# One unbroken run for the 32 narrow matmuls of each group of heads in a Mamba-2 stage

## The chip, the cores and the metric

The kernel runs on one core of a Trainium2 chip. The time is the device time of one launch in microseconds (us). A kernel is timed in several runs, and the median counts. One more execution, of the same program, is recorded by the hardware profiler; all rows below come from that record.

The engines are named as in the profile: PE is TensorE (the matmuls; PEld is its loading of weights), DVE is VectorE, ACT is ScalarE, POOL is GpSimd, SP is SyncE, which issues the DMAs here. Each engine takes its instructions in the fixed order of its own queue and waits at a semaphore where an operand or a buffer isn't ready.

## The reference

A two-layer decoder trunk on 256 tokens of width 2048, in f32. The first layer mixes with a Mamba-2 SSD block, the second with dilated sliding-window attention. Only the SSD block is touched:

```python
proj = h @ in_w
z, xBC, dt = split(proj)
xBC = silu(causal_depthwise_conv(xBC))          # width 4
xs, Bm, Cm = split(xBC)                          # 64 heads of 64, 8 groups, state 128
dt = softplus(dt + dt_bias);  A = -exp(A_log)
acum = cumsum(dt * A)                            # one chunk of 256 tokens
decay = exp(where(causal, acum[:, :, None] - acum[:, None, :], -inf))
cb = einsum("blgn,bsgn->blsg", Cm, Bm)
y = einsum("blsgk,bsgkp->blgkp", cb[..., None] * decay, xs * dt)
y = (y + xs * D_skip) * silu(z)
y = y * rsqrt(mean(y**2 per group) + eps) * norm_g
return y @ out_w
```

## The kernel before

The 256 tokens are two blocks of 128 (b = 0, 1). The 64 heads are eight groups of eight heads, g = 0 to 7. Every large product is made in f32 by three matmuls: ACT copies a weight piece of 128x1024 from `raw` to a rounded `whi` (L100), DVE makes the rest `wlo` = raw - whi (L102), and PE multiplies activation and weight in the combinations whi x hi, wlo x hi and whi x lo (L151 to L153, L182/L185, L213 to L215, three ways of tiling). The pieces arrive by DMA from SP's queue; `whi` and `wlo` have four buffers each.

The loop over the groups interleaves two things. For group g+1 it makes the projections ("bc" for every second group, "xs" for x, "z" for the gate). For group g it runs three steps:

- `stage1(g)`: two scores matmuls per group (L720, L721) into a PSUM tile `aux`, masked on DVE to `cb` (L723, L724). For each half of the heads (w = 0, 1) the rows of cumulated decay are fetched by DMA to `cbc`, ACT makes eight `Relu` (L734) and one `Exp` (L736) into `seg`, and DVE multiplies `seg` by `cb` (L737). PE transposes x (L745, four at a time, into an `aux` tile per block), and DVE makes from it `xd` (x times dt, L747), the skip term in `y` (L750) and, for block 0, `xo` (L755).
- `stage2(g)`: one matmul `po` = cb x xo (L767) into an `aux` tile. DVE scales it (L768) and adds it to y (L770). Then for each block b an output tile `py`, and for each of the eight heads two matmuls of 64 columns (L776): 32 such operations in all, each of them two records in the trace. DVE adds py to y (L777) and multiplies by the gate (L778); ACT squares with an accumulated sum (L779); DVE turns the sums into a factor (L781, L253 to L259).
- `stage3(g)`: ACT scales y by that factor (L787).

`y_tiles(g)` transposes the finished y (L829 on PE, into `aux` tiles) for the output projection, with L833 on ACT and L834 on DVE. The DVE also works through a background job, `ada_dot` (L295, one pass over 128x2048), which has nothing to do with the groups.

Buffers: `aux` (PSUM) two; `py` (PSUM) two; `seg`, `cbc` and `cb` two each; `xd` and `xo` one. So a `seg` of group g+1 can be written only when the py matmuls of group g have read it.

The order on each engine is not that of the source. A scheduler places every instruction by its priority and by estimates of when its operands are ready. `tc.issue_after(i)` obliges an instruction to be issued behind i; `tc.high_priority(n)` lifts its priority by n. Apart from these, an instruction of another product may slip between two of a loop, which is why the 32 matmuls of a group are cut in places by L213 to L215 or other work.

Of the kernel before, what the change touches and what calls it, by code (L numbers as in the profile page):

```python
# [9 lines left out]
F32 = mybir.dt.float32  # L10
# [8 lines left out]
P = 128  # L19
# [5 lines left out]
HPG = 8  # L25
# [24 lines left out]
def trunk(ctx, tc, xT, x, c, par, cst, bias, lnrow, ada, wdt, win, wxs, wout, wk, wv, wbin, wbout, out):  # L50
    nc = tc.nc
    V, S, T, PO = nc.vector, nc.scalar, nc.tensor, nc.gpsimd
# [196 lines left out]
    def rsqrt(v, tag):  # L249

        y = sm.tile(list(v.shape), F32, name=tag + "y")
        sh = sm.tile(list(v.shape), I32, name=tag + "s")
        V.tensor_scalar(sh, v.bitcast(I32), 1, None, op0=ALU.logical_shift_right)  # L253
        V.tensor_tensor(y.bitcast(I32), magic[:, :v.shape[1]], sh, op=ALU.subtract)
        t = sm.tile(list(v.shape), F32, name=tag + "t")
        for _ in range(3):
            V.tensor_tensor(t, y, y, op=ALU.mult)
            V.scalar_tensor_tensor(t, t, -0.5, v, op0=ALU.mult, op1=ALU.mult)
            V.scalar_tensor_tensor(y, t, 1.5, y, op0=ALU.add, op1=ALU.mult)  # L259
        return y  # L260
# [73 lines left out]
    with ExitStack() as cA:  # L334
# [15 lines left out]
        with ExitStack() as cS:  # L350
# [327 lines left out]
            aux2 = cS.enter_context(tc.tile_pool(name="aux2", bufs=2, space=PSUM, reuse_waits="tile"))  # L678
# [83 lines left out]
            def stage2(g, segs, xd, cb, xo):  # L762

                ss = sm.tile([P, 2], F32, name="ss")

                po = aux.tile([P, 512], F32, name="aux")
                T.matmul(po, cb[:, 2, :], xo, start=True, stop=True)  # L767
                V.tensor_tensor(xo.rearrange("p (h e) -> p h e", h=HPG), po.rearrange("p (h e) -> p h e", h=HPG),  # L768
                                dec[:, 1, g * HPG:(g + 1) * HPG, None].to_broadcast([P, HPG, 64]), op=ALU.mult)
                V.tensor_tensor(y[g][:, 1, :], xo, y[g][:, 1, :], op=ALU.add)  # L770
                for b in range(2):
                    py = aux2.tile([P, 512], F32, name="py")
                    for hh in range(HPG):
                        e_ = slice(64 * hh, 64 * hh + 64)
                        for t_ in (slice(0, 64), slice(64, 128)):
                            T.matmul(py[t_, e_], segs[hh // 4][:, hh % 4, b, t_], xd[:, b, e_], start=True, stop=True)  # L776
                    V.tensor_tensor(y[g][:, b, :], py, y[g][:, b, :], op=ALU.add)  # L777
                    V.tensor_tensor(y[g][:, b, :], y[g][:, b, :], sz[g][:, b, :], op=ALU.mult)  # L778
                    S.activation(py, y[g][:, b, :], AF.Square, accum_out=ss[:, b:b + 1])  # L779
                ms = sm.tile([P, 2], F32, name="ms")  # L780
                V.tensor_scalar(ms, ss, 1.0 / 512, EPS, op0=ALU.mult, op1=ALU.add)  # L781
                return rsqrt(ms, "a")
# [66 lines left out]
            product("z", G - 1, last_product)  # L849
            drain()  # L850
            stage3(G - 1, stage2(G - 1, *st1))
        aux = ctx.enter_context(tc.tile_pool(name="auxb", bufs=2, space=PSUM, reuse_waits="tile"))

# [197 lines left out]
    aux2 = ctx.enter_context(tc.tile_pool(name="aux3", bufs=2, space=PSUM))  # L1051
# [220 lines left out]
    _, r1, step = root(1, between)  # L1272
# [7 lines left out]
    for n, h0, h1 in ((0, 0, 512), (1, 0, 512), (3, 0, 512), (2, 0, 256), (2, 256, 512)):  # L1280
        c = slice(512 * n + h0, 512 * n + h1)
        with tc.issue_after(step.ins):
            step = V.scalar_tensor_tensor(u[1][:, c], cen[n][:, h0:h1] if n < 3 else u[1][:, c], r1, lnt[:, 1, c],
                                          op0=ALU.mult, op1=ALU.add)
# [93 lines left out]
```

## Time and profile before

| | us |
|---|---|
| median of 3 runs | 1233.01 (1232.63 to 1233.83) |
| profiled execution, its time | 1234.53 |
| its span, first to last instruction | 1232.7 |
| mean granted TensorE clock | 0.999 |
| PE busy in the span | 1216.1 (99%) |
| DVE busy | 1026.8 (83%) |
| ACT busy | 700.3 (57%) |
| SSD groups, first to last py matmul (L776) | 229.5 to 515.6 |

A row of the timeline gives the start and the duration in us, the engine, the line, the operation, out<-in with tile names, the shape and how many rows of one kind follow each other (x64); where the engine sat idle before it, the idle time and the releaser stand in brackets at the end. A row of DVE or ACT that stands for several has their common duration. Consecutive matmuls overlap in the records, so the price of one is read from start to start. In the table of windows each engine has its busy us in the stretch and the number of records.

### The profile page before, as it was taken

How to read it: one execution, taken by the hardware profiler on the slowest of the kernel's cores; microseconds unless marked ns; L12 is line 12 of the kernel's file. 1: busy time of each engine (PE TensorE's matmuls, PEld its weight loads, DVE VectorE, ACT ScalarE, POOL GpSimd, SP SyncE). 2: the span in 40 equal slices, each digit the busy share in tenths (PEclk: the TensorE clock that was granted, in tenths of full speed). 3: DMA queues.
4: the chain of work that ended last, by engine and by line, in shares of the span. 5: the costliest groups of instructions: out<-in, count | busy, mean ns of one | idle time of the engine just before them, and what ended most of it. 6: DMA issues, size and time to landing. Idle time of an engine off the chain costs nothing.

```text
span 1232.7 us, 18854 instructions
## 1 busy us (share of the span) xinstructions
PE 1216.1 (99%) x7132; PEld 1045.7 (85%) x7132; DVE 1026.8 (83%) x1464; ACT 700.3 (57%) x1048; POOL 3.9 (0%) x8
## 2 busy tenths in 40 slices
PE   8899999999999999999999999999999999999998
PEld 7889988798888888888888788888888888888886
DVE  6999986999988989899778678888978866758776
ACT  4555476878597789754435545344445644445551
POOL 0000000000000000000000000000000000000001
PEclk9999999999999999999999999999999999999999
DMA  9999976686666456599988569989997784464673
GB/s 376 423 420 423 421 256 240 217 304 242 228 207 205 169 172 207 197 339 353 362 314 302 199 204 351 357 346 371 389 395 296 228 258 150 122 197 129 206 257 69
DMA packets 81371, 335.92 MB, mean 273 GB/s; under 512 B 9200, under 2 KB 9984, under 8 KB 68480
## 3 DMA queue, kind: packets, MB, share of 16 engines
q1 hardware_dynamic: 80352, 333.33, 74.9%
q0 software_dynamic: 576, 1.05, 0.6%
q8 instruction: 56, 0.92, 0.3%
q10 hardware_dynamic: 352, 0.34, 0.1%
q14 instruction: 35, 0.29, 0.1%
HBM read 331.45 MB, written 3.23 MB: 271 GB/s over the span
## 4 chain that ended last, share of the span: by engine, by line
PE 82%; DMA 7%; DVE 6%; ACT 3%; issue 2%; ACTq 0%; DVEq 0%; SPq 0%
PE acc L182 24%; PE acc L185 12%; PE acc L214 12%; PE acc L215 11%; PE acc L213 11%; DMA raw<-in_win 5%; DVE wlo L102 2%; DVE araw L295 2%; PE py L776 1%; ACT whi L100 1%; PE acc L151 1%; PE acc L153 1%; PE acc L152 1%; PE acc L986 1%; DMA raw<-in_wv 1%
## 5 line engine op out<-in xcount | busy, mean ns | idle before, releaser
L100 ACT ACTIVATE whi<-raw 128x1024 fp32r<-128x1024 f32 x389 | 408.2, 1058 | 350.4 <-PE acc L215 127.1
L102 DVE TENSOR_TENSOR wlo<-raw,whi 128x1024 fp32r<-128x1024 f32 x389 | 468.7, 1220 | 148.2 <-ACT whi L100 140.9
L182 PE MATMUL acc<-actT,whi 128*128 128x512 f32 x1280 | 400.8, 393 | 0.0
L185 PEld LDWEIGHTS acc<-actT,wlo 128*128 128x128 f32 x1280 | 239.3, 188 | 52.3 <-DVE wlo L102 0.7
L214 PE MATMUL acc<-wlo,actT 128*128 128x512 f32 x656 | 257.4, 392 | 2.2 <-DVE wlo L102 2.2
L185 PE MATMUL acc<-actT,wlo 128*128 128x256 f32 x1280 | 254.0, 280 | 0.0
L213 PE MATMUL acc<-whi,actT 128*128 128x512 f32 x656 | 253.9, 394 | 0.0
L295 DVE SCALAR_TENSOR_TENSOR araw<-araw,cb__72 128x2048 f32<-128x2048 f32 x95 | 216.9, 2283 | 5.3 <-DMA araw<-in_ada 5.3
L182 PEld LDWEIGHTS acc<-actT,whi 128*128 128x128 f32 x1280 | 195.0, 188 | 0.4
L215 PE MATMUL acc<-whi,actT 128*128 128x512 f32 x432 | 168.8, 391 | 0.0
L214 PEld LDWEIGHTS acc<-wlo,actT 128*128 128x128 f32 x656 | 123.2, 188 | 29.5 <-DVE wlo L102 4.4
L213 PEld LDWEIGHTS acc<-whi,actT 128*128 128x128 f32 x656 | 122.6, 188 | 24.7 <-ACT s L635 0.5
L151 PE MATMUL acc<-actT,whi 128*128 128x256 f32 x372 | 103.0, 281 | 2.3 <-ACT s L635 1.3
L153 PE MATMUL acc<-actT,wlo 128*128 128x256 f32 x372 | 101.7, 281 | 1.7 <-DVE wlo L102 1.5
L152 PE MATMUL acc<-actT,whi 128*128 128x256 f32 x372 | 102.9, 279 | 0.0
L215 PEld LDWEIGHTS acc<-whi,actT 128*128 128x128 f32 x432 | 81.1, 188 | 16.6
L215 PE MATMUL acc<-whi,ylo 128*128 128x512 f32 x224 | 87.5, 391 | 0.0
L151 PEld LDWEIGHTS acc<-actT,whi 128*128 128x128 f32 x372 | 69.6, 188 | 3.6 <-ACT s L635 1.7
L153 PEld LDWEIGHTS acc<-actT,wlo 128*128 128x128 f32 x372 | 68.8, 188 | 2.9 <-DVE wlo L102 2.9
L152 PEld LDWEIGHTS acc<-actT,whi 128*128 128x128 f32 x372 | 70.6, 190 | 0.2
L215 PEld LDWEIGHTS acc<-whi,ylo 128*128 128x128 f32 x224 | 42.1, 188 | 8.4
L734 ACT ACTIVATE seg<-cbc,cumT 128x128 f32<-128x128 f32 x128 | 41.1, 389 | 4.1 <-PE py L776 2.1
(311 smaller groups left out, 1147.4 us busy)
## 6 DMA issues: line engine op xcount, KB each, us to landing
araw<-in_ada SPq DMA_DIRECT2D x96, 1024.0 KB, 7.0
raw<-in_win SPq DMA_DIRECT2D x109, 512.0 KB, 6.2
raw<-in_wout SPq DMA_DIRECT2D x64, 512.0 KB, 5.5
raw<-in_wbin SPq DMA_DIRECT2D x64, 512.0 KB, 4.3
raw<-in_wxs SPq DMA_DIRECT2D x48, 512.0 KB, 4.4
raw<-in_wv SPq DMA_DIRECT2D x48, 512.0 KB, 6.3
raw<-in_wk SPq DMA_DIRECT2D x48, 512.0 KB, 7.3
cbc<-cumd SPq DMA_DIRECT2D x16, 512.0 KB, 5.0
```

Source lines behind the costliest of these rows:

```text
L100: copied.append(S.activation(hi, raw, AF.Copy))
L102: latest.append(V.tensor_tensor(lo, raw, hi.bitcast(F32), op=ALU.subtract))
L151: T.matmul(o, hi[:, k, c_], ahi[:, kt, :], start=first, stop=False, skip_group_check=True)
L152: T.matmul(o, hi[:, k, c_], alo[:, kt, :], start=False, stop=False, skip_group_check=True)
L153: T.matmul(o, lo[:, k, c_], ahi[:, kt, :], start=False, stop=kt == k1 - 1, skip_group_check=True)
L182: T.matmul(ps[n], hi[:, k, n * P:n * P + P], both(kt), start=kt == 0, stop=False, skip_group_check=True)
L185: T.matmul(ps[n][:, 0, :], lo[:, k, n * P:n * P + P], high(kt), start=False, stop=kt == KT - 1, skip_group_check=True)
L213: T.matmul(o, h_, hi[:, k, :], start=kt == k0, stop=False, skip_group_check=part)
L214: T.matmul(o, h_, lo[:, k, :], start=False, stop=False, skip_group_check=part)
L215: end = T.matmul(o, l_, hi[:, k, :], start=False, stop=kt == k1 - 1, skip_group_check=part)
L295: return V.scalar_tensor_tensor(raw, raw, 1.0, cb_, op0=ALU.mult, op1=ALU.mult, accum_out=mod[layer][:, ct, j:j + 1])
L734: S.activation(seg[:, hh, b, :], cbc[:, hh, b, :], AF.Relu, bias=cumT[:, b, h0 + hh:h0 + hh + 1], scale=-1.0)
```

## The change

Both py tiles of a group are allocated ahead of the matmuls. The 32 matmuls are issued block 1 first, then block 0, and the heads from the last to the first. Each is obliged to come behind the one before it, the first behind the `po` matmul, and all of them have a priority raised by 400. The sums on DVE and ACT follow in the order block 1, block 0, after all matmuls have been written.

```diff
--- before.py
+++ after.py
@@ -764,16 +764,20 @@
                 ss = sm.tile([P, 2], F32, name="ss")
 
                 po = aux.tile([P, 512], F32, name="aux")
-                T.matmul(po, cb[:, 2, :], xo, start=True, stop=True)
+                step = T.matmul(po, cb[:, 2, :], xo, start=True, stop=True)
                 V.tensor_tensor(xo.rearrange("p (h e) -> p h e", h=HPG), po.rearrange("p (h e) -> p h e", h=HPG),
                                 dec[:, 1, g * HPG:(g + 1) * HPG, None].to_broadcast([P, HPG, 64]), op=ALU.mult)
                 V.tensor_tensor(y[g][:, 1, :], xo, y[g][:, 1, :], op=ALU.add)
-                for b in range(2):
-                    py = aux2.tile([P, 512], F32, name="py")
-                    for hh in range(HPG):
+                pys = {b: aux2.tile([P, 512], F32, name="py") for b in (1, 0)}
+                for b in (1, 0):
+                    for hh in reversed(range(HPG)):
                         e_ = slice(64 * hh, 64 * hh + 64)
                         for t_ in (slice(0, 64), slice(64, 128)):
-                            T.matmul(py[t_, e_], segs[hh // 4][:, hh % 4, b, t_], xd[:, b, e_], start=True, stop=True)
+                            with tc.issue_after(step.ins), tc.high_priority(400):
+                                step = T.matmul(pys[b][t_, e_], segs[hh // 4][:, hh % 4, b, t_], xd[:, b, e_],
+                                                start=True, stop=True)
+                for b in (1, 0):
+                    py = pys[b]
                     V.tensor_tensor(y[g][:, b, :], py, y[g][:, b, :], op=ALU.add)
                     V.tensor_tensor(y[g][:, b, :], y[g][:, b, :], sz[g][:, b, :], op=ALU.mult)
                     S.activation(py, y[g][:, b, :], AF.Square, accum_out=ss[:, b:b + 1])
```

The lines behind it move down: L776 becomes L777, L777 becomes L781, L778 L782, L779 L783, L781 L785, L829 L833, L833 L837, L834 L838. The instructions are the same in number, apart from two more loads of ACT's function table (the program's order has 1024 ACT instructions, it had 1022). What changes lies between group 0 and the end of group 7; ahead of it and behind it every engine's order is as before. On PE, the runs of L776 were 15 and 17 long in group 0 (po between them), 19 and 13 in group 2, 3 and 29 in groups 3 and 4, 12 and 20 in group 7, and 32 in groups 1, 5 and 6; now all eight are 32, each directly behind its po.

The first place is group 2. On PE, the po of group 2 and the products around it (acc_3338 and acc_3339 are the z projection of group 3; whi_3354, whi_3372 and whi_3390 are three of its weight pieces in turn), before:

```order
L215 MATMUL acc_3339<-whi_3372,actT_84 128x512
L213 MATMUL acc_3338<-whi_3390,actT_84 128x512
L213 MATMUL acc_3339<-whi_3390,actT_84 128x512
L767 MATMUL aux_3488<-xo_3329,cb_3292 128x512
L776 MATMUL py_3492<-xd_3321,seg_3297 64x64 x8
L776 MATMUL py_3492<-xd_3321,seg_3310 64x64 x8
L776 MATMUL py_3512<-xd_3321,seg_3297 64x64 x3
L214 MATMUL acc_3338<-wlo_3391,actT_84 128x512
L215 MATMUL acc_3338<-whi_3390,actT_84 128x512
L214 MATMUL acc_3339<-wlo_3391,actT_84 128x512
L215 MATMUL acc_3339<-whi_3390,actT_84 128x512
```

and now:

```order
L215 MATMUL acc_3339<-whi_3354,actT_84 128x512
L213 MATMUL acc_3338<-whi_3372,actT_84 128x512
L213 MATMUL acc_3339<-whi_3372,actT_84 128x512
L767 MATMUL aux_3488<-xo_3329,cb_3292 128x512
L777 MATMUL py_3492<-xd_3321,seg_3310 64x64 x8
L777 MATMUL py_3492<-xd_3321,seg_3297 64x64 x8
L777 MATMUL py_3493<-xd_3321,seg_3310 64x64 x8
L777 MATMUL py_3493<-xd_3321,seg_3297 64x64 x8
L214 MATMUL acc_3338<-wlo_3373,actT_84 128x512
L215 MATMUL acc_3338<-whi_3372,actT_84 128x512
L214 MATMUL acc_3339<-wlo_3373,actT_84 128x512
```

The po has come forward by four L213, four L214 and four L215, and the 13 matmuls that stood further down are now part of the run. On DVE in the stretch that leads to the same group's xo (xo_3329 comes further down, at the end of group 2's L747, L750 and L755; araw is the background job), before:

```order
L102 TENSOR_TENSOR wlo_3355<-raw_3352,whi_3354 128x1024
L295 SCALAR_TENSOR_TENSOR araw_3610,mod0_80<-araw_3610,cb__72 128x2048
L102 TENSOR_TENSOR wlo_3373<-raw_3370,whi_3372 128x1024
L191 TENSOR_TENSOR xs_3071<-acc_3178,xs_3071 128x256
L191 TENSOR_TENSOR xs_3071<-acc_3179,xs_3071 128x256
L723 TENSOR_TENSOR cb_3292<-aux_3289,cc_76 128x256
L368 SCALAR_TENSOR_TENSOR cacc_3275<-xs_3071,prm_74,cacc_3275 128x255
```

and now:

```order
L102 TENSOR_TENSOR wlo_3355<-raw_3352,whi_3354 128x1024
L295 SCALAR_TENSOR_TENSOR araw_3937,mod0_80<-araw_3937,cb__72 128x2048
L723 TENSOR_TENSOR cb_3292<-aux_3289,cc_76 128x256
L191 TENSOR_TENSOR xs_3071<-acc_3178,xs_3071 128x256
L191 TENSOR_TENSOR xs_3071<-acc_3179,xs_3071 128x256
L724 COPY cb_3292<-aux_3289 128x128
L737 TENSOR_TENSOR seg_3297<-seg_3297,cb_3292 128x1024
```

The piece wlo_3373 has gone behind the group's own work, and the background pass that stands here is a later one (araw_3937 for araw_3610): from group 0's L768 to the xo of group 2 there are 7 passes of L295 for 6 before, and 24 of L102 for 25. In group 1 the run with its po has gone back by 12 L182 and 10 L185 matmuls; between the L781 of group 0 and the xo of group 1, DVE has 4 L295 for 2, 14 L102 for 12, 24 L368 for 18 and 4 L191 for 2, since the two L745 blocks of that group stand later too.

The second place is the entry to group 5, on ACT (seg_4787 and seg_4800 are group 5's, py_4417 and py_4437 group 4's, whi_4584 a weight piece of the product that runs then), before:

```order
L100 ACTIVATE whi_4501<-raw_4499 128x1024
L100 ACTIVATE whi_4507<-raw_4505 128x1024
L100 ACTIVATE whi_4584<-raw_4582 128x1024
L414 ACTIVATE sz_4407<-s7_101 128x512
L734 ACTIVATE seg_4787<-cbc_4785,cumT_104 128x128
L414 ACTIVATE sz_4407<-s7_101 128x512
L734 ACTIVATE seg_4787<-cbc_4785,cumT_104 128x128 x7
L779 ACTIVATE py_4417,ss_4412<-s4_98 128x512
L779 ACTIVATE py_4437,ss_4412<-s4_98 128x512
L100 ACTIVATE whi_4606<-raw_4604 128x1024
```

and now:

```order
L734 ACTIVATE seg_4787<-cbc_4785,cumT_104 128x128 x8
L734 ACTIVATE seg_4800<-cbc_4798,cumT_104 128x128
L736 ACT_TABLE_LOAD
L736 ACTIVATE seg_4787<-seg_4787 128x1024
L414 ACT_TABLE_LOAD
L414 ACTIVATE sz_4407<-s7_101 128x512 x2
L783 ACTIVATE py_4417,ss_4412<-s4_98 128x512
L783 ACTIVATE py_4418,ss_4412<-s4_98 128x512
L365 ACTIVATE cacc_4538<-s5_99,prm_74 128x256
L365 ACTIVATE cacc_4544<-s5_99,prm_74 128x256
L365 ACTIVATE cacc_4551<-s5_99,prm_74 128x256
L100 ACTIVATE whi_4584<-raw_4582 128x1024
```

The nine Relu, the Exp and two table loads stand now ahead of whi_4584. On DVE the matching wlo_4585 has gone behind seven of the L368 (the convolution). On PE the L720, the L721 and four L745 of group 5 have come forward, to stand behind the first two L182 of whi_4584.

The third place is the passage from group 6 to group 7. On PE (aux_5309, aux_5342 and aux_5351 are group 7's scores and its two transposed blocks; acc_5275 and acc_5276 are the z projection of group 7), before:

```order
L214 MATMUL acc_5276<-wlo_5292,actT_84 128x512
L215 MATMUL acc_5276<-whi_5291,actT_84 128x512
L720 MATMUL aux_5309<-bcm_4550 128x2x128
L721 MATMUL aux_5309<-bcm_4550 128x128
L745 MATMUL aux_5342<-cc_76,xs_4950 128x128 x4
L213 MATMUL acc_5275<-whi_5360,actT_84 128x512
L214 MATMUL acc_5275<-wlo_5361,actT_84 128x512
L215 MATMUL acc_5275<-whi_5360,actT_84 128x512
L745 MATMUL aux_5351<-cc_76,xs_4950 128x128 x4
```

and now:

```order
L214 MATMUL acc_5275<-wlo_5361,actT_84 128x512
L215 MATMUL acc_5275<-whi_5360,actT_84 128x512
L767 MATMUL aux_5215<-xo_5205,cb_5168 128x512
L777 MATMUL py_5219<-xd_5197,seg_5186 64x64 x8
L777 MATMUL py_5219<-xd_5197,seg_5173 64x64 x8
L777 MATMUL py_5220<-xd_5197,seg_5186 64x64 x8
L777 MATMUL py_5220<-xd_5197,seg_5173 64x64 x8
L720 MATMUL aux_5309<-bcm_4550 128x2x128
L721 MATMUL aux_5309<-bcm_4550 128x128
L745 MATMUL aux_5342<-cc_76,xs_4950 128x128 x4
```

The run of group 6 (xd_5197) with its po has gone back by 33 matmuls (11 each of L213, L214 and L215) and stands now directly ahead of group 7's scores; before, it stood where the z projection begins. Further down, the L829 of `y_tiles(0)` (aux_5414 and aux_5423) follow each other with the first use of wlo_5397 behind them, and the 12 py matmuls of group 7 that stood between are gone from there. On ACT (seg_5317 and seg_5330 are group 7's), before:

```order
L734 ACTIVATE seg_5317<-cbc_5315,cumT_104 128x128 x6
L370 ACTIVATE xs_4950<-cacc_5151 128x256
L370 ACTIVATE xs_4950<-cacc_5157 128x256
L734 ACTIVATE seg_5317<-cbc_5315,cumT_104 128x128 x2
L734 ACTIVATE seg_5330<-cbc_5328,cumT_104 128x128
L736 ACT_TABLE_LOAD
L736 ACTIVATE seg_5317<-seg_5317 128x1024
L779 ACTIVATE py_5219,ss_5214<-s6_100 128x512
L734 ACTIVATE seg_5330<-cbc_5328,cumT_104 128x128 x3
L779 ACTIVATE py_5239,ss_5214<-s6_100 128x512
L734 ACTIVATE seg_5330<-cbc_5328,cumT_104 128x128 x4
L100 ACTIVATE whi_5396<-raw_5394 128x1024
```

and now:

```order
L100 ACTIVATE whi_5434<-raw_5432 128x1024
L734 ACTIVATE seg_5317<-cbc_5315,cumT_104 128x128 x8
L734 ACTIVATE seg_5330<-cbc_5328,cumT_104 128x128
L736 ACT_TABLE_LOAD
L736 ACTIVATE seg_5317<-seg_5317 128x1024
L783 ACTIVATE py_5219,ss_5214<-s6_100 128x512
L783 ACTIVATE py_5220,ss_5214<-s6_100 128x512
L734 ACTIVATE seg_5330<-cbc_5328,cumT_104 128x128 x7
L837 ACTIVATE xs_5412<-aux_5414,prm_74 128x256
L736 ACTIVATE seg_5330<-seg_5330 128x1024
L837 ACTIVATE xs_5412<-aux_5423,prm_74 128x256
```

whi_5396 and whi_5434 come now ahead of the nine Relu, and the Exp of seg_5330 behind an L833 (now L837). On DVE, wlo_5397 stands behind L755 of block 0 and L747 and L750 of block 1 as before, but ahead of the second L737.

## The prediction

> **What bounds the kernel.** I read the page's busy times first, then the table of windows, then what PE waits for, and last the timelines of PE, DVE and ACT around each group's narrow matmuls.
>
> ```profile
> span 1232.7 us, 18854 instructions
> PE 1216.1 (99%) x7132; PEld 1045.7 (85%) x7132; DVE 1026.8 (83%) x1464; ACT 700.3 (57%) x1048; POOL 3.9 (0%) x8
> ...
> 225.00:520.00 295.00, 295.00 (x2052) 252.12 (x2051) 273.06 (x470) 233.07 (x403) 0.00 (x0) 1.00 0.62 211
> 520.00:700.00 180.00, 179.45 (x817) 147.59 (x816) 146.72 (x180) 81.40 (x102) 0.00 (x0) 1.00 0.87 317
> 700.00:1233.00 533.00, 528.42 (x2877) 453.32 (x2875) 416.79 (x572) 254.12 (x361) 3.67 (x4) 1.00 0.73 254
> ```
>
> In the second window, where all eight groups lie, PE is busy for 295.00 of 295.00 us: it waits for nothing, so nothing that the change makes arrive earlier can shorten it. Only matmuls that get cheaper can, and every new wait of PE costs its full length, because behind 520 us PE is again busy for 707.87 of 713 us and has next to no slack to give it back. DVE, at 273.06 us, has 22 us to spare in the same window, and those are not spread evenly.
>
> **What is saved: the breaks.** The 32 operations are 64 records. Group 4 has a short piece of them and then the rest, group 6 an unbroken run:
>
> ```profile
> 414.87 1.02 PE L767 MATMUL aux<-xo,cb 128*128 128x512 f32 x2
> 415.82 0.45 PE L776 MATMUL py<-xd,seg 128*64 128x64 f32 x6
> 416.19 0.50 PE L214 MATMUL acc<-wlo,actT 128*128 128x512 f32 x1
> 416.53 0.40 PE L215 MATMUL acc<-whi,actT 128*128 128x512 f32 x1
> 416.77 0.40 PE L214 MATMUL acc<-wlo,actT 128*128 128x512 f32 x1
> ...
> 418.40 0.40 PE L215 MATMUL acc<-whi,actT 128*128 128x512 f32 x1
> 418.72 1.96 PE L776 MATMUL py<-xd,seg 128*64 128x64 f32 x58
> ...
> 485.80 2.09 PE L776 MATMUL py<-xd,seg 128*64 128x64 f32 x64
> 487.82 0.50 PE L213 MATMUL acc<-whi,actT 128*128 128x512 f32 x1
> ```
>
> The 64 of group 6 take 2.02 us from start to start of what follows, 32 ns each. The plain pace of a 512-wide matmul is 0.23 to 0.24 us (416.53 to 416.77). The last L215 ahead of the second piece takes 0.32 (418.40 to 418.72), the L214 behind the first 0.34 (416.19 to 416.53), and the six records take 0.37 (415.82 to 416.19) where 6 x 0.032 is 0.19. So a break costs 0.09 ahead, 0.11 behind and 0.10 to 0.18 in the piece, 0.30 to 0.38 us. The upper end counts the start of a run as well, which stays, so I take 0.30. Four pieces merge (groups 2, 3, 4 and 7): 4 x 0.30 = **1.2 us** saved, at most 1.5. Group 0's break by its po (15 and 17) is worth 0.1 to 0.2, and the L721 that the new order puts far behind its L720 costs about as much; I set both to nothing. Reversing heads and blocks changes neither number nor shape: nothing.
>
> The Trainium skill, page "TensorEngine Tiling (Array Packing)", section Key Properties, says that changing the tiling mode drains TensorE, and gives no figure. The trace agrees in kind: the L214 behind a piece takes 0.34 us. By that rule the gain would be what the rows give, 1.2 us, or more if a drain is hidden from them, which is a rival below.
>
> **What is added: waits.** The raised priority places a whole run where one piece stood, and moves others. I went through each group and asked whether xo (for the po) and the weight pieces behind the run are there.
>
> *Groups 1 and 2.*
>
> ```profile
> 246.16 0.17 DVE L781 TENSOR_SCALAR ms<-ss 128x2 f32<-128x2 f32 x1 [0.94 <-ACT py L779]
> 246.24 2.29 DVE L295 SCALAR_TENSOR_TENSOR araw<-araw,cb__72 128x2048 f32<-128x2048 f32 x1
> ...
> 278.02 0.68 DVE L755 TENSOR_TENSOR xo<-aux,dec 128x512 f32<-128x512 f32 x1
> ...
> 317.76 0.68 DVE L755 TENSOR_TENSOR xo<-aux,dec 128x512 f32<-128x512 f32 x1
> ...
> 319.55 4.62 DVE L102 TENSOR_TENSOR wlo<-raw,whi 128x1024 fp32r<-128x1024 f32 x4
> ...
> 324.98 1.23 DVE L102 TENSOR_TENSOR wlo<-raw,whi 128x1024 fp32r<-128x1024 f32 x1 [0.21 <-ACT whi L100]
> ...
> 485.74 0.76 DVE L191 TENSOR_TENSOR xs<-acc,xs 128x256 f32<-128x256 f32 x2
> ...
> 487.01 2.44 DVE L368 SCALAR_TENSOR_TENSOR cacc<-xs,prm,cacc 128x255 f32<-128x255 f32 x6
> ...
> 283.46 1.02 PE L767 MATMUL aux<-xo,cb 128*128 128x512 f32 x2
> 318.99 1.02 PE L767 MATMUL aux<-xo,cb 128*128 128x512 f32 x2
> ```
>
> Between 246.16 and 324.98 DVE has no bracket of idle time: 79 us in which its times are sums of its own work. Up to group 2's xo the new order gives it one L295 more (2.28) and one L102 less (4.62 / 4 = 1.15): xo ends at 318.44 + 1.13 = 319.6. The wait of 0.94 us at 246.16 is for an L779, which in the new order stands ahead of three Relu (0.3 each) and not behind them; it may end 0.85 earlier, and then xo at 318.7. PE reaches that po twelve 512-wide matmuls earlier, at 318.99 - 12 x 0.23 = 316.2. The wait is 2.5 to 3.4 us. I take **2.6**, near the lower end, since the order does have that L779 ahead. Up to 1.1 of it falls to group 1 already: there DVE has two L295, two L102, six L368 and two L191 more ahead of xo (4.6 + 2.3 + 2.4 + 0.7 = 10.0; 278.70 becomes 288.6, or 287.8), and PE comes 12 L182 and 10 half as wide L185 later (2.8 + 1.2; 283.46 becomes 287.4). The two waits are one: DVE is behind by what it is behind at group 2, and PE loses it there or earlier.
>
> *Groups 0, 3, 4 and 6.* Group 0's run has no piece ahead of the po any more and waits 0.1 for xo. In 3 and 4 the order ahead of the po is unchanged, and PE didn't wait there. In 6 the po comes 33 matmuls later (7.6 us, at 492.4) and xo, on DVE, at 492 by the same kind of sum. I take **0.1** in all.
>
> *Group 5's entry.*
>
> ```profile
> 421.12 2.15 ACT L734 ACTIVATE seg<-cbc,cumT 128x128 f32<-128x128 f32 x7
> 423.18 0.58 ACT L779 ACTIVATE py<-s 128x512 f32<-128x512 f32 x1
> ...
> 425.47 1.28 ACT L736 ACT_TABLE_LOAD   x1
> 426.76 1.06 ACT L736 ACTIVATE seg<-seg 128x1024 f32<-128x1024 f32 x1
> 427.73 1.57 ACT L365 ACTIVATE cacc<-s,prm 128x256 f32<-128x256 f32 x3
> ...
> 428.93 0.62 PE L182 MATMUL acc<-actT,whi 128*128 128x512 f32 x2
> 429.39 0.40 PE L185 MATMUL acc<-actT,wlo 128*128 128x256 f32 x2
> ...
> 493.41 0.59 PE L720 MATMUL aux<-bcm 128*128 128x256 f32 x2
> ...
> 494.42 0.48 PE L213 MATMUL acc<-whi,actT 128*128 128x512 f32 x1
> ```
>
> The run of group 4 ends near 417.8 (414.87 + 0.95 + 2.0) and frees its seg. From there ACT has nine Relu (2.7), two table loads (2.6), an Exp (1.0), two L414 (1.0, of L779's shape), two L779 (1.2), three L365 (1.5) and then the copy whi_4584 (1.0): 11.0 us, to 428.8, where PE wants it at 428.93 less the 0.3 of a break saved. On DVE wlo_4585 now stands behind seven L368, which begin when the first L365 ends, near 426.9: 2.8, small steps 0.5, itself 1.15, so it ends at 431.3. PE wants it at 429.39, later by the 1.0 of the L720, L721 and four L745 put ahead of it (493.41 to 494.42), earlier by the 0.3: 430.1. I take **1.0**, since ACT costs PE 0.1 to 0.2 of that before; 0.6 to 1.9 as ends, by whether L365 comes on time.
>
> *Group 7.* This is the largest term.
>
> ```profile
> 487.47 1.87 ACT L734 ACTIVATE seg<-cbc,cumT 128x128 f32<-128x128 f32 x6 [0.18 <-PE py L776]
> ...
> 497.34 0.68 DVE L755 TENSOR_TENSOR xo<-aux,dec 128x512 f32<-128x512 f32 x1
> ...
> 500.55 1.22 DVE L102 TENSOR_TENSOR wlo<-raw,whi 128x1024 fp32r<-128x1024 f32 x1
> ...
> 500.88 0.60 PE L829 MATMUL aux<-cc,s 128*128 128x128 f32 x4
> 501.41 0.92 PE L776 MATMUL py<-xd,seg 128*64 128x64 f32 x24
> 502.25 0.50 PE L214 MATMUL acc<-wlo,actT 128*128 128x512 f32 x1
> ```
>
> The first row's bracket shows the mechanism: the Relu of group 7 begin when the run of group 6 has read seg. That run now ends 33 matmuls later, at 487.82 + 33 x 0.23 = 495.4, but what it holds up is wanted where it was. Nine Relu, a table load and the Exp make 5.0: seg is there at 500.4. DVE's L737 (of L102's shape, 1.15) ends at 501.6, L781 and L755 at 502.4, which frees the aux tile for the first L829; L747 and L750 at 503.7 free the second; and wlo_5397 (1.15) ends at 504.9. PE, without the 12 py ahead (501.41 to 502.25), would want it at 501.4. The wait is **3.5** us in two or three stretches; with the roundings of eleven terms 3.0 to 3.9. The 20 and 12 py of group 7 stand together at the later place, where xo is long there.
>
> **The sum.** Waits 2.6 + 0.1 + 1.0 + 3.5 = 7.2, breaks -1.2: +6.0 us. The profiled execution took 1234.53, 1.5 above the median; from it the sum gives 1240.5, from the median 1233.01 it gives **1239.0** (+0.5%). What a measurement of this kernel can tell from no change is 0.2%, 2.5 us.
>
> **Rivals.**
>
> - *Only the breaks count.* DVE and ACT might get their new order at no cost to PE: PE would then go at 1233.0 - 1.2 = 1231.8, no change that can be told. It speaks for it that DVE has 22 us to spare in the window; against it, that at both large places the rows show DVE without idle time, or ACT released by the run itself. It decides at 316.2 us (xo of group 2) and 501.4 us (wlo_5397).
> - *Breaks are dearer than I read* (the other side). Thirteen pieces become eight. If each that goes costs 0.8 us or more rather than 0.3, as a drain of the array that shows later than in the neighbouring rows, and data are in time, five fewer give 4.0 us: 1229.0. Below 0.5 each it stays within 2.5 us. Against it: the rows behind a break return to 0.24 within one matmul.
> - *Only group 7 waits.* If DVE is early in groups 1 and 2 (L295 held back by its own DMA) and ACT in 5, what is left is 3.5 - 1.2: 1235.3.
> - *More waits.* The upper ends, 3.4 + 0.1 + 1.9 + 3.9 = 9.3, less 1.2, give 1241.1; with four further weight pieces late by group 5's lower end, 0.6 each, 1243.5.
> - *The clock falls in a wait.* Were the clock halved for as long as the longest wait, 3.5 us, another 1.8 us would go: 1240.8. This row, in which PE is busy for 1.89 of 4 us, shows 1.00:
>
> ```profile
> 222.00:226.00 4.00, 1.89 (x11) 1.48 (x11) 4.00 (x10) 3.37 (x5) 0.00 (x0) 1.00 0.62 236
> ```
>
> The Trainium skill, page "TensorE: Matmul & The Clock Gate", section "Part 1: The HAM clock gate", halves the clock after an idle window of about 3.4 us. By that rule the 2.1 us of this row were too short to show it, and group 7's wait, cut by L829, would be too.
>
> **Chances.** The forecast, 1236 to 1241.5: 0.50. Group 7 alone or parts, 1234 to 1236: 0.17, of which about half under +2.5. More waits or the clock, over 1241.5: 0.10. Breaks alone: 0.10. Dearer breaks: 0.13. So faster 0.13; same 0.10 + 0.07 = 0.17; slower 0.70. The range leaves out the dearer breaks (under 1230.5) and the far end above 1243 (0.06): 1230.5 to 1243.0; the likeliest's own is 1236 to 1241.5.
>
> **What would show it.** Right: L776 (now L777) in eight runs of 64 records; waits of PE for L755 at the po of groups 1 and 2, of 2 to 3 us together; a wait ahead of the second L185 piece at 430; after 495 the Relu of group 7 released by py, then PE waiting at L829 and for wlo L102; the clock at 1.00. Wrong: PE busy for all of the window, or the window shorter than 295 us by more than 1.5; DVE idle ahead of group 2's xo; or the time lost elsewhere, above all behind 520 us, where I expect nothing.

## The result and the profile after

The changed kernel takes 1242.0 us, median of 6 runs (1240.22 to 1244.39), against 1232.9 us before (6 runs, 1232.29 to 1234.12): ratio 1.0071, 95% interval 1.0061 to 1.0082 (a ratio is taken over the runs; the quotient of the two medians would be 1.0074). It is slower by 9.1 us; the forecast was +6.0, in a range that reached to 1243.0. Medians and ratios below leave out two runs of later kernels that took far longer than all others, 1504.68 and 4317.72 us; with them two of the medians would be 1237.49 and 1232.68. The profiled execution took 1240.22, the fastest of the six. Its busy times and windows (the SSD groups end some 7 us later, so the windows are moved):

```profile
span 1238.4 us, 18854 instructions
PE 1218.2 (98%) x7132; PEld 1047.6 (85%) x7132; DVE 1029.0 (83%) x1464; ACT 704.7 (57%) x1050; POOL 3.9 (0%) x8
...
225.00:527.00 302.00, 294.95 (x2047) 251.51 (x2047) 273.37 (x467) 235.90 (x405) 0.00 (x0) 0.99 0.63 208
527.00:706.00 179.00, 178.45 (x811) 146.80 (x810) 146.07 (x181) 80.81 (x99) 0.00 (x0) 1.00 0.86 314
706.00:1239.00 533.00, 528.12 (x2875) 453.20 (x2874) 416.52 (x570) 253.90 (x360) 3.67 (x4) 1.00 0.73 254
```

In the last two windows PE idles as long as before to 0.3 us; all of the loss lies in the first. To measure it I take two places that both orders share: the first L213 behind group 0's two L745 blocks (at 224.71 us before, 222.00 now) and the first transpose behind group 7's run (the L829 at 515.57, now the L833 at 521.56). PE takes 290.9 us from one to the other before and 299.6 now, 8.7 more. The two profiled executions as a whole differ by only 5.7, because the one before had lost 2.7 ahead of this stretch, most of it in one wait at an L745 (2.11 us, here 0.33). In the first window PE now idles for 7.05 of 302 us, where it had no idle time, and its mean clock is 0.99. What it waited for in that window (engine, tile, line <- releaser: us, times, longest):

```profile
PE aux L767 <- DVE xo L755: 2.7, 2, 2.6
PE aux L833 <- DVE as L253: 1.2, 1, 1.2
PE aux L833 <- DVE at L257: 0.9, 1, 0.9
PE acc L185 <- DVE wlo L102: 0.8, 1, 0.8
PE acc L214 <- DVE wlo L102: 0.7, 1, 0.7
PE acc L151 <- ACT whi L100: 0.7, 1, 0.7
```

The places are those of the prediction: the po of groups 1 and 2, the entry to group 5, the y transposes ahead of group 7 (L829, now L833), and 0.7 us at group 0. This last one is not the wait that the prediction named there: it had 0.1 for xo, but an L151 that now stands ahead of the po waits for its whi. The releasers "as L253" and "at L257" are the small DVE steps that happen to stand behind L755 and L750, which free the aux tiles. The rows on PE, and on ACT the Relu of group 7, which begin when group 6's run has ended:

```profile
317.16 1.10 PE L767 MATMUL aux<-xo,cb 128*128 128x512 f32 x2 [2.58 <-DVE xo L755]
...
431.26 0.50 PE L185 MATMUL acc<-actT,wlo 128*128 128x256 f32 x2 [0.78 <-DVE wlo L102]
...
503.12 0.41 PE L833 MATMUL aux<-cc,s 128*128 128x128 f32 x2 [1.21 <-DVE as L253]
504.45 0.41 PE L833 MATMUL aux<-cc,s 128*128 128x128 f32 x2 [0.93 <-DVE at L257]
505.56 0.50 PE L214 MATMUL acc<-wlo,actT 128*128 128x512 f32 x1 [0.70 <-DVE wlo L102]
...
507.04 0.63 PE L214 MATMUL acc<-wlo,actT 128*128 128x512 f32 x1
507.47 0.63 PE L215 MATMUL acc<-whi,actT 128*128 128x512 f32 x1
...
495.84 2.74 ACT L734 ACTIVATE seg<-cbc,cumT 128x128 f32<-128x128 f32 x9 [3.40 <-PE py L777]
```

The two rows at 507 are what I had not put into the sum: 0.43 us from start to start where 0.23 is the pace. After group 7's waits the clock fell, where the prediction had named a clock of 1.00 as a sign of being right (window: us, PE, PEld, DVE, ACT, POOL busy, clock, DMA):

```profile
500.00:505.00 5.00, 2.73 (x15) 1.70 (x13) 4.84 (x11) 5.00 (x14) 0.00 (x0) 1.00 0.01 2
505.00:510.00 5.00, 4.44 (x15) 3.56 (x15) 5.00 (x11) 3.37 (x5) 0.00 (x0) 0.66 0.37 105
```

In windows of 1 us it is 0.78, 0.50, 0.50 and 0.51 from 506 to 510, and 1.00 on either side.

### The profile page after: what moved, and what is told of

It is laid out like the page before. It is cut to its first block, busy times and chain, and to the rows that moved or that the text cites. A ratio compares the mean times of both kernels' runs of the same rounds, so it can differ in the third digit from the quotient of the medians.

```text
span 1238.4 us, 18854 instructions
## 1 busy us (share of the span) xinstructions
PE 1218.2 (98%) x7132; PEld 1047.6 (85%) x7132; DVE 1029.0 (83%) x1464; ACT 704.7 (57%) x1050; POOL 3.9 (0%) x8
## 4 chain that ended last, share of the span: by engine, by line
PE 79%; DVE 8%; DMA 8%; ACT 3%; issue 2%; DVEq 0%; ACTq 0%; SPq 0%
PE acc L182 23%; PE acc L185 12%; PE acc L214 11%; PE acc L215 11%; PE acc L213 11%; DMA raw<-in_win 5%; DVE wlo L102 3%; DVE araw L295 2%; DVE cacc L368 1%; PE py L777 1%; ACT whi L100 1%; DMA araw<-in_ada 1%; PE acc L153 1%; PE acc L151 1%; PE acc L152 1%
## 5 line engine op out<-in xcount | busy, mean ns | idle before, releaser
L102 DVE TENSOR_TENSOR wlo<-raw,whi 128x1024 fp32r<-128x1024 f32 x389 | 468.4, 1221 | 140.9 <-ACT whi L100 135.3
L182 PE MATMUL acc<-actT,whi 128*128 128x512 f32 x1280 | 400.7, 393 | 0.0
L185 PEld LDWEIGHTS acc<-actT,wlo 128*128 128x128 f32 x1280 | 239.1, 188 | 53.0 <-DVE wlo L102 1.4
L214 PE MATMUL acc<-wlo,actT 128*128 128x512 f32 x656 | 257.8, 393 | 3.0 <-DVE wlo L102 3.0
L185 PE MATMUL acc<-actT,wlo 128*128 128x256 f32 x1280 | 254.1, 280 | 0.8 <-DVE wlo L102 0.8
L213 PE MATMUL acc<-whi,actT 128*128 128x512 f32 x656 | 253.6, 394 | 0.0
L295 DVE SCALAR_TENSOR_TENSOR araw<-araw,cb__72 128x2048 f32<-128x2048 f32 x95 | 217.0, 2284 | 3.8 <-DMA araw<-in_ada 3.6
L182 PEld LDWEIGHTS acc<-actT,whi 128*128 128x128 f32 x1280 | 195.2, 188 | 0.6
L215 PE MATMUL acc<-whi,actT 128*128 128x512 f32 x432 | 169.5, 392 | 0.0
L214 PEld LDWEIGHTS acc<-wlo,actT 128*128 128x128 f32 x656 | 123.5, 188 | 30.4 <-DVE wlo L102 5.0
L213 PEld LDWEIGHTS acc<-whi,actT 128*128 128x128 f32 x656 | 122.8, 188 | 24.5 <-ACT s L635 0.5
L151 PE MATMUL acc<-actT,whi 128*128 128x256 f32 x372 | 102.9, 280 | 2.2 <-ACT actT L502 0.9
L215 PEld LDWEIGHTS acc<-whi,actT 128*128 128x128 f32 x432 | 81.4, 188 | 16.6
L215 PE MATMUL acc<-whi,ylo 128*128 128x512 f32 x224 | 87.8, 392 | 0.0
L151 PEld LDWEIGHTS acc<-actT,whi 128*128 128x128 f32 x372 | 69.6, 188 | 3.7 <-ACT actT L502 1.3
L215 PEld LDWEIGHTS acc<-whi,ylo 128*128 128x128 f32 x224 | 42.1, 188 | 8.5
```

What stands on the lines that cost most here:

```text
L102: latest.append(V.tensor_tensor(lo, raw, hi.bitcast(F32), op=ALU.subtract))
L151: T.matmul(o, hi[:, k, c_], ahi[:, kt, :], start=first, stop=False, skip_group_check=True)
L182: T.matmul(ps[n], hi[:, k, n * P:n * P + P], both(kt), start=kt == 0, stop=False, skip_group_check=True)
L185: T.matmul(ps[n][:, 0, :], lo[:, k, n * P:n * P + P], high(kt), start=False, stop=kt == KT - 1, skip_group_check=True)
L213: T.matmul(o, h_, hi[:, k, :], start=kt == k0, stop=False, skip_group_check=part)
L214: T.matmul(o, h_, lo[:, k, :], start=False, stop=False, skip_group_check=part)
```

## The experiments

Two theories stood against each other. The waits: the unbroken run is worth its breaks, and the time goes into waits of PE for data that the moved instructions made late. The run itself: to issue all 32 at once, with both py tiles and seg held to its end, costs about 1.1 us a group. Times beside each kernel are of the same chip.

**Old order of blocks and heads, in all groups.** Chain, priority and early allocation stay:

```diff
-                pys = {b: aux2.tile([P, 512], F32, name="py") for b in (1, 0)}
-                for b in (1, 0):
-                    for hh in reversed(range(HPG)):
+                pys = {b: aux2.tile([P, 512], F32, name="py") for b in (0, 1)}
+                for b in (0, 1):
+                    for hh in range(HPG):
...
-                for b in (1, 0):
+                for b in (0, 1):
                     py = pys[b]
```

> The changed kernel with its unbroken run, its chain and its raised priority, but block 0 and head 0 first as before. PE's order has the same eight runs of 32; the run of group 6 stands again where it stood before the change, DVE has 4 background passes instead of 6 between group 0 and the xo of group 2, and the copy ahead of group 5's L182 comes ahead of the Relu again. Theory (the time went into waits of PE for late data, and the run itself saves the breaks): no wait over 0.5 us at group 2's po, at group 5's entry and at group 7's y transposes, five breaks saved at 0.17 us each: 1232.3 us, between 1231.3 and 1233.5. Rival (the unbroken run itself costs, by both py tiles and seg being held to its end): 1240 to 1243 like the change.

Measured: 1232.72 us against 1232.84, ratio 0.9999 (0.9990 to 1.0008). All eight runs are unbroken and nothing that can be told is lost: the theory of the run itself falls. Between the two places of the section above PE takes 291.3 us here, 290.9 before. The window has no wait at group 2 and a full clock:

```profile
225.00:527.00 302.00, 300.29 (x2086) 257.11 (x2085) 280.07 (x489) 238.77 (x412) 0.00 (x0) 1.00 0.65 218
```

This trace gives the price of the breaks as well. I summed, from the end of group 0's run to the stage's end, what PE's steps from start to start take above the plain pace of their shape, single steps over 0.25 us left out: 3.07 us before, 1.63 here. The stretch holds four of the five merges (groups 2, 3, 4 and 7; group 0's lies ahead of it), so the 1.44 us saved are 0.36 for each, as far as the plain pace can be told. The steps left out (0.4 at group 1's po, 0.25 at an L745, 0.9 ahead of an L214 near 499, which is over the 0.5 expected at that place) sum to 1.5 and take the gain back, with the 0.7 at group 0, which stands here too.

**Without the raised priority.** The changed kernel, second block first, chained:

```diff
-                            with tc.issue_after(step.ins), tc.high_priority(400):
+                            with tc.issue_after(step.ins):
```

> The changed kernel (second block first, last head first, chained) without the raised priority. The runs are 23 and 9, 32, 32, 3 and 29, 3 and 29, 32, 32, 32; group 6's run stands where it stood before, and group 2's xo is early on DVE. Theory of the waits: no wait over 0.5 us in groups 2, 5 and 7, two breaks saved: 1232.6 us, between 1231.5 and 1234. Rival (the reversed order itself costs, since the run begins with the seg half that is ready last): 1236 or more, with PE waiting for the second L737 ahead of the runs.

Measured: 1234.45 against 1232.84, ratio 1.0014 (1.0005 to 1.0023). The three large waits are gone as expected, but the time is 1.6 above before, outside my range. Its trace has single steps of 0.6 at 298.6 and 0.5 at 503.1, 0.7 of waiting at 229.9, and the breaks of groups 0, 3 and 4. These make some 1.5; that they are the whole of it isn't shown. What this run does show is that the reversed order without the raised priority makes none of the three large waits.

**Unbroken in groups 3, 4 and 7 alone.** The kernel before, with chain and priority (old order of blocks) where g is 3, 4 or 7:

```diff
-                T.matmul(po, cb[:, 2, :], xo, start=True, stop=True)
+                step = T.matmul(po, cb[:, 2, :], xo, start=True, stop=True)
...
-                            T.matmul(py[t_, e_], segs[hh // 4][:, hh % 4, b, t_], xd[:, b, e_], start=True, stop=True)
+                            with (tc.issue_after(step.ins) if g in (3, 4, 7) else ExitStack()), (tc.high_priority(400) if g in (3, 4, 7) else ExitStack()):
+                                step = T.matmul(py[t_, e_], segs[hh // 4][:, hh % 4, b, t_], xd[:, b, e_], start=True, stop=True)
```

> The kernel before with chain and priority in groups 3, 4 and 7 alone, blocks and heads in the old order. Groups 0 to 2 stand as before; 3, 4 and 7 have one run of 32 each. Theory of the waits: nothing waits, three breaks saved: 1232.4 us, between 1231.3 and 1233.5. Rival (the unbroken run itself costs about 1.1 us a group): 1236.3.

Measured: 1232.60 against 1232.84, ratio 0.9998 (0.9989 to 1.0008). The same sum over small steps is 2.26 for 3.07: 0.27 us for each of three breaks, and waits of 1.1 beside it.

**A third seg buffer.** The changed kernel with

```diff
-                    seg = px.tile([P, 4, 2, P], F32, name="seg")
+                    seg = px.tile([P, 4, 2, P], F32, name="seg", bufs=3)
```

> The changed kernel with a third seg buffer. The run of group 6 stands late as in the change, but the Relu of group 7 need not wait for it. The order of groups 1 and 2 shifts: by sums over DVE's order the xo of group 1 is 0.8 us late and that of group 2 early. Theory of the waits: PE's wait at group 7's y transposes (3.3 us and the clock's fall behind it) is gone, the one at group 5's entry stays at 0.9: 1233.9 us, between 1232.8 and 1236. Rival (the late run of group 6 costs by itself, not by the seg buffers): the wait ahead of L833 stays and the time is 1237 or more.

Measured: 1240.06 against 1232.84, ratio 1.0064 (1.0050 to 1.0078): my expectation was wrong by 6 us. By its own signs the rival came true: a wait ahead of L833 stayed, and the time is over 1237. Group 2's wait is gone, as the sums had it, but the one at group 7 has grown:

```profile
494.81 2.45 ACT L734 ACTIVATE seg<-cbc,cumT 128x128 f32<-128x128 f32 x8 [3.40 <-PE py L777]
...
500.84 1.06 ACT L736 ACTIVATE seg<-seg 128x1024 f32<-128x1024 f32 x1
...
501.93 1.23 DVE L737 TENSOR_TENSOR seg<-seg,cb 128x1024 f32<-128x1024 f32 x1
503.07 0.15 DVE L258 SCALAR_TENSOR_TENSOR at<-at,ms 128x2 f32<-128x2 f32 x1
503.14 0.68 DVE L747 TENSOR_TENSOR xd<-aux,dtT 128x512 f32<-128x512 f32 x1
...
501.89 0.41 PE L833 MATMUL aux<-cc,s 128*128 128x128 f32 x2 [1.02 <-DVE at L257]
504.64 0.41 PE L833 MATMUL aux<-cc,s 128*128 128x128 f32 x2 [2.34 <-DVE at L257]
```

One buffer more frees one half of the heads. The other half's eight Relu still wait for group 6's run, and in this order DVE does that half's L737 ahead of the L747 that reads the second aux tile, so PE waits 2.34 us there. DVE has a second chain besides: the sums of group 6 (L781, L782) come behind the late run as well and hold DVE to 499.0 in the changed kernel, where its L737 then waits only 0.15 us for the Exp. So the late run costs through more than the seg buffers, which is the rival's point. The clock falls here as well, to 0.50 from 506 to 508. Whether four seg buffers would help is open; no run has them.

**One place cured at a time.** The next two kernels have the old order of blocks and heads in a single group, all else as changed:

```diff
-                for b in (1, 0):
-                    for hh in reversed(range(HPG)):
+                for b in ((0, 1) if g == 1 else (1, 0)):
+                    for hh in (range(HPG) if g == 1 else reversed(range(HPG))):
```

with the two other loops over b to match. In group 1:

> The changed kernel with block 0 and head 0 first in group 1 alone. PE's order from group 2 on is that of the change, with group 2's po at the same place; DVE has two background passes, one wlo, six L368 and two L191 less between group 0 and the xo of group 2 (8.7 us by sums), so that xo is there in time. Theory of the waits: the 2.6 us ahead of group 2's po are gone, those at group 5's entry (0.8) and group 7 (2.8, and the clock behind it 1.7) stay: before + 0.3 + 0.8 + 3.3 + 1.7 - 0.85 = 1238.1 us, between 1236.5 and 1239.5. Rival (group 2's wait costs nothing that isn't got back later, all of the loss being group 7 and the clock): 1241 or more.

Measured: 1238.95 against 1232.88, ratio 1.0054 (1.0040 to 1.0068), within the theory's range and below the rival's. In group 4 (g == 4 in the same places):

> The changed kernel with block 0 and head 0 first in group 4 alone. The order up to group 4 is that of the change, with group 2's late xo; behind it, whi_4584 comes again ahead of most Relu, and group 6's run stands again 33 matmuls earlier. Theory of the waits: the 2.6 us ahead of group 2's po stay, those at group 5's entry and group 7 go, and the clock's fall with them: before + 0.3 + 2.7 - 0.85 = 1235.0 us, between 1234 and 1237 (the upper end if the clock falls at group 2 in some runs). Rival (all eight unbroken runs with the reversed order cost alike): 1241 or more.

Measured: 1237.42 against 1232.88, ratio 1.0033 (1.0021 to 1.0045), above the theory's 1235.0 and just above its range. PE's rows, the first three with group 1 in the old order, the last three and the windows with group 4:

```profile
314.59 1.02 PE L767 MATMUL aux<-xo,cb 128*128 128x512 f32 x2
...
500.51 0.41 PE L833 MATMUL aux<-cc,s 128*128 128x128 f32 x2 [1.21 <-DVE as L253]
501.84 0.66 PE L833 MATMUL aux<-cc,s 128*128 128x128 f32 x2 [0.93 <-DVE at L257]
```

```profile
318.47 2.05 PE L767 MATMUL aux<-xo,cb 128*128 128x512 f32 x2 [2.55 <-DVE xo L755]
...
503.51 0.60 PE L833 MATMUL aux<-cc,s 128*128 128x128 f32 x4
504.64 0.50 PE L214 MATMUL acc<-wlo,actT 128*128 128x512 f32 x1 [0.53 <-DVE wlo L102]
315.00:320.00 5.00, 2.45 (x7) 0.92 (x5) 5.00 (x8) 2.95 (x4) 0.00 (x0) 0.82 0.00 0
320.00:325.00 5.00, 5.00 (x74) 4.14 (x74) 5.00 (x6) 2.38 (x9) 0.00 (x0) 0.84 0.59 187
```

Each cure takes away its own waits and leaves the others. In the second kernel the clock falls behind group 2's wait of 2.55 us (the two records of L767 take twice as long), which it had not done in the change's profiled execution; one of its runs kept a mean clock of 1.000 and took 1235.69, the others, at 0.996 to 0.998, 1237.0 to 1237.7. So most of the miss is one fall of the clock, some 1.7 us. The mean clock of a run is a rough guide here, because it also holds falls at the kernel's start: the first 50 us show 0.97 in this profile and in the one before.

**The clock by itself.** Behind the end of the kernel before, bursts of matmuls with waits of a known length between:

```diff
...
+    def matmuls(n):
+        nonlocal step
+        for i in range(n):
+            with tc.issue_after(step.ins):
+                step = T.matmul(banks[i % 2], stat, w, start=True, stop=True)
+
+    def wait(m):
+        nonlocal step
+        for i in range(m):
+            with tc.issue_after(step.ins):
+                step = V.tensor_tensor(w, cb_[:, :512], cb_[:, 512:1024], op=ALU.mult)
+
+    for turn in range(4):
+        for m in range(1, 10):
+            matmuls(43 + (5 * m + 3 * turn) % 8)
+            wait(m)
+        matmuls(45 + turn)
+        wait(2)
+        matmuls(2)
+        wait(2)
+        matmuls(2)
+        wait(1)
...
```

> The kernel before with a bench behind its end: four turns of nine bursts of 43 to 50 matmuls (512 wide, about 10 us a burst), each followed by a wait of PE for one to nine multiplications on DVE (about 0.6 us each), and at each turn's end a wait cut in three by two pairs of matmuls, as at group 7's y transposes. The bench's results are not used. Theory (the clock is halved for some 3.4 us after a stretch in which PE idles enough, however it is cut): the cut wait and the single waits over about 3 us are followed by rows at half the clock in most turns, a wait under 2 us never, and each fall costs 1.7 us more than the wait. Rival (only a single wait of 3.4 us or more makes it fall): the cut wait is followed by full clock in all four turns.

It ran once, under the profiler. The cut wait of the first turn, and its windows:

```profile
1379.12 0.73 PE L1294 MATMUL acc<-s,s 128*128 128x512 f32 x2 [1.51 <-DVE s L1300]
1381.36 0.73 PE L1294 MATMUL acc<-s,s 128*128 128x512 f32 x2 [1.51 <-DVE s L1300]
1382.88 7.34 PE L1294 MATMUL acc<-s,s 128*128 128x512 f32 x24 [0.78 <-DVE s L1300]
...
1380.00:1385.00 5.00, 2.86 (x8) 1.94 (x9) 1.96 (x3) 0.00 (x0) 0.00 (x0) 0.81 0.01 3
1385.00:1390.00 5.00, 5.00 (x20) 4.09 (x19) 0.00 (x0) 0.00 (x0) 0.00 (x0) 0.84 0.00 0
```

Counted over all four turns (the record of one execution), a fall being a burst that takes over 1 us more than its plain pace:

| wait of PE, us | bursts with a fall | extra us in the burst behind it |
|---|---|---|
| 0.8, 1.5 | 0 of 8 | 0.1 |
| 2.24 | 1 of 4 | 1.7 |
| 2.96 | 2 of 4 | 1.7, 2.9 |
| 3.69 | 1 of 4 | 2.6 |
| 4.4 to 6.6 | 16 of 16 | 1.5 to 2.9 |
| cut: 1.51, 1.51, 0.78 | 4 of 4 | 1.4 to 3.0 |

The rival falls: the cut wait, no part of which lasted over 1.51 us, was followed by a fall in every turn, in the third already behind its first pair of matmuls. The expected line of about 3 us for single waits is not there: 2.24 did it once, and 3.69 didn't three times. A fall isn't always 1.7 us either.

The trace's record of the granted clock shows why the same wait falls or doesn't. The 24 falls of the bench all begin a whole number of 3.413 us apart, and last 3.41, 6.83 or, once, 10.24 us: the clock is set on a grid of its own, which doesn't follow the waits. So I cut the traces into the windows of their grid; what PE idles in one is its width less PE's busy time, the figure behind it. The rows are, in pairs of neighbouring windows, one of the bench's waits of 3.69 us, and a longer one; then group 2's wait in the change's first profiled execution, and in the later one (further down):

```profile
1448.00:1451.41 3.41, 1.47 (x7) 0.89 (x5) 1.83 (x3) 0.00 (x0) 0.00 (x0) 1.00 0.00 0
1451.41:1454.83 3.42, 1.67 (x7) 1.41 (x8) 1.62 (x3) 0.00 (x0) 0.00 (x0) 1.00 0.00 0
...
1321.71:1325.12 3.41, 1.38 (x7) 0.80 (x5) 1.93 (x3) 0.00 (x0) 0.00 (x0) 1.00 0.00 0
1325.12:1328.53 3.41, 0.31 (x1) 0.31 (x2) 2.91 (x5) 0.00 (x0) 0.00 (x0) 0.50 0.00 0
...
315.42:318.83 3.41, 1.67 (x24) 0.94 (x26) 3.41 (x6) 1.31 (x3) 0.00 (x0) 1.00 0.00 0
318.83:322.24 3.41, 3.41 (x59) 3.00 (x56) 3.41 (x4) 2.39 (x9) 0.00 (x0) 1.00 0.49 139
...
316.04:319.45 3.41, 1.04 (x5) 0.54 (x3) 3.41 (x7) 2.95 (x4) 0.00 (x0) 1.00 0.00 0
319.45:322.86 3.41, 3.23 (x26) 1.75 (x28) 3.41 (x5) 0.00 (x0) 0.00 (x0) 0.50 0.03 4
```

The wait of 3.69 us is split into 1.94 and 1.75 us of idling, and the clock stays; the longer one has 2.03 in its first window, and the clock falls. Group 2's wait of 2.58 us had 1.74 in its larger window and kept the clock; in the later execution the 2.55 us have 2.37 in one window, and it falls.

**Both cures, and the change again.** The old order in groups 1 and 4, `g in (1, 4)` in the places shown:

> The changed kernel with block 0 and head 0 first in groups 1 and 4, the other six as in the change. Theory of the waits: both late places are cured together, and what is left of the change is five breaks saved (1.4 us by the trace of the kernel with the old order throughout) and some 1.5 us of small waits: 1232.8 us, between 1231.8 and 1234.0. Rival (the reversed order costs in each of the other six groups too, a share that the two single cures could not show): 1234.5 or more.

Measured: 1232.41 against 1232.66, ratio 0.9999 (0.9990 to 1.0008). And the changed kernel on the same chip:

> The changed kernel itself once more, on the same chip as the kernel cured in groups 1 and 4, to see whether the two cures add up. From the kernels cured in one place each (1238.95 with group 2's wait gone, 1237.49 with those of groups 5 and 7 gone, before 1232.88), the two losses are 6.1 and 4.6; each of them holds the saved breaks less the small waits, about 0 net. Theory (the waits and the clock's falls add): before + 10.7 = 1243.6 us, between 1241 and 1245, the runs differing by the number of falls, with mean clocks of 0.994 to 0.998. Rival (the falls of the clock don't add, one takes the place of the other): 1241.5 or less with a mean clock of 0.998.

Measured: 1243.57 (1240.86 to 1244.85), ratio 1.0079 (1.0065 to 1.0093), with mean clocks of 0.998, 0.997, 0.995, 0.995 and 0.994 from the fastest run to the slowest. The two losses add in three of the five runs; the two fastest, 1240.86 and 1241.14, are as short as the rival had it. In this profile the clock falls twice in the groups, behind group 2's wait and behind group 7's:

```profile
319.63 2.04 PE L767 MATMUL aux<-xo,cb 128*128 128x512 f32 x2 [2.55 <-DVE xo L755]
...
320.00:325.00 5.00, 5.00 (x70) 3.29 (x70) 5.00 (x6) 1.17 (x4) 0.00 (x0) 0.71 0.37 116
510.00:515.00 5.00, 5.00 (x18) 3.83 (x17) 4.32 (x11) 3.36 (x5) 0.00 (x0) 0.66 0.36 105
```

No version here beats the kernel before by what a measurement can tell: the breaks are worth some 1.4 us, 0.1%.

## Why the prediction was right, and where it was not

The direction, the places and the size of the three large waits were forecast. The time was not: 1242.0 lies above the forecast's own 1236 to 1241.5, where the prediction had put "more waits or the clock" with a chance of 0.10. In the table the measured column is the change's profiled execution, waits counted from start to start against the plain pace (the brackets show somewhat less, since ends are modelled).

| term | forecast, us | measured, us |
|---|---|---|
| breaks saved | -1.2 | -1.4 (from the old order's trace) |
| groups 1 and 2, xo late | 2.6 | 0.3 + 2.7 |
| groups 0, 3, 4 and 6 | 0.1 | 0.9, all at group 0, for another operand |
| entry to group 5, wlo late | 1.0 | 0.9 |
| group 7, aux tiles and wlo late | 3.5 | 1.4 + 1.1 + 0.9 = 3.3 |
| clock | 0 | 1.7 for each fall of 3.41 us: one in this execution, two in the later one |
| sum | 6.0 | 8.4 with one fall; the stretch of the groups shows 8.7 |

- *The bound and the order of things.* PE had no slack in the window, so every wait counted in full, and nothing over 0.3 us came back behind it. The sums over DVE's and ACT's order gave each of the three large waits within 0.5 us.
- *The terms that were mis-sized* are the clock, above all, and group 0. I set the clock to nothing on a row in which 2.1 us of waiting left it at 1.00, and held group 7's wait to be harmless because L829 cuts it. But that row's wait had only 1.87 us in one window of its grid (222.46 to 225.87), and so was no test. In the traces the clock falls behind group 2's wait in two of the three executions that have it, and behind group 7's cut wait in all four executions that have it, the third seg buffer's among them. The waits without the clock come to 6.7 us, so some 2.4 of the 9.1 are left for the falls and the spread of the runs (4.2 us, before 1.8). How these two share it isn't shown: one of the six runs kept a mean clock of 1.000, which leaves no room for a fall in the groups (3.41 us at half the clock would make it 0.999), and still took 1240.51. By a rule of the Trainium skill, page "TensorE: Matmul & The Clock Gate", section "Part 1: The HAM clock gate", the gate looks at activity in a free-running window of 3.4 us and re-throttles after an idle one. The runs agree on the half clock, on its some 3.4 us, and on the chance in it; they differ on "idle", since a window with two short bursts in it, or a wait of 2.24 us, sufficed, and some falls last two or three windows.
- *Rivals.* "Only the breaks count" and "dearer breaks" are refuted as accounts of this change, and so is "only group 7 waits". As a price, the 0.30 us a break of the sum held, at 0.27 to 0.36: eight unbroken runs without the waits give 1232.4 to 1232.7, not 1229.
- *The cause was put in one part of the change; it takes two.* I wrote that the raised priority moves the runs and that reversing blocks and heads costs nothing. With the old order, chain and priority cost nothing that can be told; with the reversed order and no raised priority the three large waits are gone; and with both, taking the reversed order out of groups 1 and 4 removes the whole loss. So the large waits come from the reversed order in these two groups together with the priority. No instruction's price has changed: the two move what the scheduler puts ahead of group 2's xo on DVE, and where it puts group 6's run. By what rule it does so, whether blocks or heads matter, and whether the reversed order in groups 1 and 4 alone would make the same loss, no run shows.
- *Group 7's mechanism* was right in its trigger (the Relu released by group 6's py, 3.40 us of ACT's waiting) and incomplete: a third seg buffer did not end it, since half the Relu and DVE's own sums hang on the same run.

## What to carry to other kernels

Where one engine is busy throughout, a reordering of small instructions is worth what it saves on that engine alone, here 0.3 us a break, and is lost by the first operand that comes late elsewhere; sum the other engines' queues up to each operand that the moved work needs. Change a loop's order and its constraints apart, in one iteration at a time: here the order in two of eight groups, together with the priority, cost all of it. A wait of TensorE over about 2 us can have a second price, and several short waits close together are to be counted as one.

## What the runs showed of the hardware

Behind a wait of PE the clock can fall to 0.50, for 3.41, 6.83 or 10.24 us, which costs 1.4 to 3.0 us more in the burst behind it. In the bench it never did so behind single waits up to 1.51 us, in 4 of 12 cases behind 2.24 to 3.69 us, in all 16 behind 4.4 us and more, and in all four behind 3.8 us of idling cut by two pairs of matmuls.

What decides is how the wait lies in the grid of 3.41 us. With the clock at 1.00, every window of the bench that had 2.03 us or more of one wait was followed by a fall, and no window with 1.94 us or less of one; from 20 us on, no window of the other traces here, but for cut waits, goes against that. A wait of 2.24 us can lie in one window, and one of 4.41 leaves 2.2 in one of two. Where short matmuls cut the wait, less was enough by the records: 1.7 us in the bench, and 1.6 at group 7's y transposes. These are counts of these traces, with PE's ends modelled.
